# Two transformer layers on one core: late down-weight splits behind the last gate tile, three modulation units a pair, the residual's copy issued by GpSimd

## Chip, core and metric

One Trainium2 chip, one of its cores. The kernel is one launch; the metric is device time in microseconds, the median of repeated runs. A core has five engines that run their own instruction queues strictly in order: TensorE (PE, with its weight loads shown as PEld), VectorE (DVE), ScalarE (ACT), GpSimd (POOL) and SyncE (SP, which here only issues DMAs). They wait for each other by semaphores.

## The reference

Two layers of a diffusion backbone with 512 latent tokens and 256 context tokens, 1024 features. Each layer modulates a normalised stream by vectors made from a conditioning vector, attends, projects, adds a gated residual, and then does the same with a SwiGLU of 2816 hidden features. The second layer gives no context output. Cut to what matters here:

```python
for l in range(DEPTH):                       # 2 layers
    sh_a, sc_a, g_a, sh_f, sc_f, g_f = split(silu(c) @ mod_w[l] + mod_b[l], 6)
    # the context stream has the same six from c_ctx
    a_lat, a_ctx = modulate(h_lat, sh_a, sc_a), modulate(h_ctx, csh_a, csc_a)
    o_lat, o_ctx = mixer(a_lat, a_ctx)       # layer 0: two kinds of heads; layer 1: sliding window
    h_lat = h_lat + g_a * o_lat
    h_lat = h_lat + g_f * swiglu(modulate(h_lat, sh_f, sc_f), w_gate_up[l], w_down[l])
    # the context stream likewise in layer 0 only
return rms_norm(h_lat, final_norm)

def swiglu(h, w_gate_up, w_down):
    g, u = split(h @ w_gate_up, 2)
    return (silu(g) * u) @ w_down
```

## The kernel before

**Layout and precision.** Activations lie transposed: 128 features on the partitions, tokens along the free dimension, so a stream is 8 tiles of 128 x 768 (latent tokens 0 to 511, context 512 to 767). Every float32 operand of a matmul is split into a rounded high part (a cast on ACT) and the rest (a subtraction on DVE), and a product is three matmuls: high x high, high x low, low x high. So each weight panel costs a DMA, a cast and a split before TensorE can use it: `load_w` (cast L311, split L312) or `parts` (cast L1248, split L1249).

**Who sets the order.** The program is written in the order of the mathematics; a planner that simulates a timeline then gives each engine its queue, earlier program text having the higher priority. `behind` (an ordering dependency that costs no semaphore) fixes the order of two instructions of one engine by hand. What the planner has fixed, the engine obeys: if the first instruction of its queue waits for a DMA, everything behind it waits.

**Buffers.** Tiles come from tagged pools with a fixed number of buffers, taken in the order of the program: `wr` (raw weights, 3), `wh`, `wl` (their split, 3 each), `nb` (2), `st` (12), `b` (24), `p` (8), `rope0` (1). A load into a tag goes out when the buffer's last readers are done.

**Layer 0's FFN.** `ffn` walks 22 pairs (gate and up panel j of 128 hidden features) in chunks of 4, 4, 4, 4, 3, 3; after a chunk come its down products for all eight output panels m. Pairs 0 and 1 are plain; the others (`Pair`) use a seven-product scheme in which tokens (halves of 384) and feature halves are combined. Pair j's `head` and `body` come first, then the `tail` of the pair before, so a tail closes a gate tile: two products of 12 matmuls (L1261 to L1263), the Silu on ACT (L1316), the add (L1318), two times gate x up (L1320) on DVE, and cast and split (L1248, L1249) of the hidden tile, which the down products read.

**Modulation units.** Behind pair j stand `bg(more(j))` units of the generator `all_mods`. The first four in the FFN are column products of layer 0's last vector (`mods_pe`), in pairs 0 to 3. The next 48 are layer 1's tiles (`mod_tile` in its late form): POOL issues a load of 128 x 1024 into the one `rope0` buffer (L215), DVE multiplies and sums it against the conditioning vector (L220), for the first 16 tiles twice (both streams).

**The last chunk.** Pairs 19, 20, 21. `final0` fetches the old residual (8 loads by POOL, L1116) and calls `output`: for m = 0 to 7 it gets a down panel of 128 x 384 by `kept_w` (raw in `wr`, split in `nb` for m = 0 and 1, in `st` after that), does nine matmuls for the latent tokens (L322, L324, L325), and the residual's add on DVE (L1112); then the same panels for the context tokens. The sums of squares for layer 1's norm run along (ACT L356, adds L359 on POOL and DVE), then the sum over partitions on TensorE (L373), the root on ACT (L375), the spread (L382) and the modulation (L407 to L409). `kept_w` also loads the first three panels of layer 1's input projection into the list `soon` (L311, L312).

**Behind it.** The latent residual is written to HBM (`parked`, eight DMAs of 256 KB, L1413) so that its buffers can be used; layer 1's key, value and first query products (L763 to L765) follow, and the rotary embedding, whose multiplications run on POOL (L456 to L458).

Of the kernel before, what the change touches and what calls it, by code (L numbers as in the profile page):

```python
# [12 lines left out]
ALU = mybir.AluOpType  # L13

P = 128
D = 1024
KT = D // P
# [10 lines left out]
CHUNKS = ((0, 4), (4, 4), (8, 4), (12, 4), (16, 3), (19, 3)), ((0, 3), (3, 3), (6, 4), (10, 4), (14, 4), (18, 4))  # L28
MLA_SCALE = 96.0 ** -0.5
LOWEST = -3.0e38  # L30
LATS = slice(0, NL)
# [37 lines left out]
LOWER = 150  # L69
LOE = {(0, 2, 0): None, (0, 2, 1): None, (0, 5, 0): None, (0, 5, 1): 1, (1, 2, 0): None, (1, 2, 1): None, (1, 5, 0): None, (1, 5, 1): None}  # L70
PATTERN = ("fbsfbsfbbsfs",) * 3
BG = ((0, 0, 0, 0, 0), (2, 3), (0, 0), (0, 0))
FIRST = 2000
STEPS = ((2, 3, 4, 4), 5, 3)
HALVES = (slice(0, 256), slice(256, 512))
# [25 lines left out]
def hybrid_kernel(ctx: ExitStack, tc, I, out):  # L101
# [6 lines left out]
    def T(tag, shape, dt=F32):  # L108
        count[0] += 1
        if tag not in SIZES:  # L110
            return sb.tile(shape, dt, tag=tag, name=f"{tag}_{count[0]}", bufs=BUFS.get(tag, 1))
        n = int(np.prod(shape[1:]))
        t = sb.tile([P, SIZES[tag] // (2 if dt == mybir.dt.bfloat16 else 4)], dt, tag=tag, name=f"{tag}_{count[0]}",
                    bufs=BUFS[tag])[: shape[0], :n]
        if len(shape) == 3:
            t = t.rearrange("p (a b) -> p a b", a=shape[1])
        return t

    def B(dt=F32, tag="b"):
        return T(tag, [P, NT], dt)  # L120
# [12 lines left out]
    def dma(o, i):  # L133
        return nc.sync.dma_start(f(o), f(i))

    V, S, G, PE = nc.vector, nc.scalar, nc.gpsimd, nc.tensor

    def f(ap):
        return ap.bitcast(F32) if ap.dtype == F32R else ap
# [155 lines left out]
    def bg(n=1):  # L295

        for _ in range(n):
            next(mods, None)
# [7 lines left out]
    def load_w(src, kt, m, eng=None, tag=None, after=()):  # L306

        r = T("wr", [P, kt * m])
        dma(r, src)
        h, lo = (B(F32R, tag)[:, : kt * m] if tag else T(x, [P, kt * m], F32R) for x in ("wh", "wl"))  # L310
        behind(S.copy(h, r), *after[:1])  # L311
        behind((G if eng else V).tensor_tensor(lo, r, f(h), op=ALU.subtract), *after[1:])  # L312
        return tuple(x.rearrange("p (k m) -> p k m", k=kt) for x in (h, lo))
# [48 lines left out]
    marks = {}  # L362
# [75 lines left out]
    def modulated(src, l, comp, eng=None, two=None):  # L438

        res, done = [], []  # L440

        def use(k, r, c, v):
            if k == len(res):
                res.append((B(F32R), B(F32R)))
            done.append(modulate(res[k], src[k], k, r, l, comp, v, c, eng, done[-2:-1]))

        return Norm(src, use, eng, two=two), res
# [72 lines left out]
    def behind(ins, *before):  # L520

        for x in before:
            tc.add_manual_dep(ins.ins, x.ins.name, mybir.DependencyInfo(mybir.DependencyClass.NoSync,
                              mybir.DependencyReason.DATA), reason="products in one run")
        return ins
# [227 lines left out]
    r = B(tag="nb")  # L753
# [78 lines left out]
    def beside(gen):  # L832
        side_work.append(gen)
        return gen
# [79 lines left out]
    def split_pair(p):  # L914

        tag = ("b", "st")[p - 2]
        q, k = raws[2 * p - 4 : 2 * p - 2]
        how = S.copy, G.tensor_copy, V.tensor_copy
        sets.append((new_q(tag), new_k(tag)))
        put_q(sets[p][0], None, how[RQ[p - 2]], (G, V)[RL[p - 2]])(q, slice(0, NT))  # L920
        yield
        put_k(sets[p][1], KC[1], how[RK[p - 2]])(k, slice(0, NT))
        yield
# [63 lines left out]
    def latent_operands(h):  # L987
        p, s = divmod(h, 2)
        r, u = NOPE[s], USED[s]
        rr = slice(32 * (h % 4), 32 * (h % 4) + 32)  # L990
        if p < 2:
            if p == 0:
                KA.append([T("st", [P, NT], F32R) for _ in range(2)])
            QA[s].append([T("st", [P, NT], F32R) for _ in range(2)])
            for t in [*(KA[s] if p == 0 else ()), *QA[s][p]] if s else ():
                (V if "z" in EV else G).memset(f(t[:32]), 0.0)
            if p == 0:
                for i in range(2):
                    V.tensor_copy(KA[s][i][ROPE[s]], KR[i][:32])
        (ka, kc), (qa, qb) = KA[s], QA[s][p % 2]  # L1000
        for x, (hi, lo) in ((kn[p], (ka, kc)), (qn[p], (qa, qb))):
            S.copy(hi[r], x[r])
            (V if "l" in EV and p < 1 else G).tensor_tensor(lo[r], x[r], f(hi[r]), op=ALU.subtract)
        for t, x in zip((qa, qb), QR[h // 4]):
            if "d" in EV:
                dma(t[ROPE[s]], x[rr])
            else:
                G.dma_start(t[ROPE[s]], x[rr])

        def scores(o, q, keys):  # L1010
            q = slice(q * P, (q + 1) * P)
            PE.matmul(o, qa[u, q], ka[u, keys], start=True, stop=False)
            PE.matmul(o, qb[u, q], ka[u, keys], start=False, stop=False)
            PE.matmul(o, qa[u, q], kc[u, keys], start=False, stop=True)

        return scores
# [12 lines left out]
    def na_jobs():  # L1029
        for p in range(4):  # L1030
            if p == 3:
                lower[0] = L3
            for x in ORDER[p]:
                beside(split_pair(int(x)) if x in "23" else {"n": latent_norms, "m": mla_prepare}[x]())
            rate[0] = STEPS[0][p], BG[0][p]
            if p % 2 == 0:
# [34 lines left out]
    def mla_jobs():  # L1071
        phase[0], lower[0] = 1, LOWER
        rate[0] = STEPS[1], BG[0][4]
        ready.append(latent_operands(1))
# [23 lines left out]
    H = []  # L1098
    for k in range(KT):
        t = B()  # L1100
# [13 lines left out]
    def fetched(m, c, tag="p"):  # L1114
        t = B(tag=tag)
        G.dma_start(t[:, c], home[m][:, c])  # L1116
        return t

    ahead, soon = {}, []

    def kept_w(src, m):

        if 2 < m < 6:
            soon.append(load_w(I["w_in1"][(8, 9, 0)[m - 3]], KT, P))
        if m in ahead:
            return ahead[m]
        r, t = T("wr", [P, 384]), T("nb", [P, NT], F32R) if m < 2 else B(F32R, "st")
        dma(r, src(m))
        return tuple(x.rearrange("p (k m) -> p k m", k=3) for x in parts(r, t[:, :384], t[:, 384:]))

    def output(src, mov, l, comp, streams, norm, units, dst=None, keep=False, base=None, wait=0):

# [112 lines left out]
        return Norm(src, use, G if l else None, (0, 4, 1, 5, 2, 6, 3, 7)), ops, sums  # L1245

    def parts(t, h, lo, after=()):
        S.copy(h, t)  # L1248
        behind(V.tensor_tensor(lo, t, f(h), op=ALU.subtract), *after)  # L1249
        return h, lo  # L1250

    norm, ops, sums = combined(H, 0, 3, TOK1, TOK2)
    output(lambda m: I["w_out0"][m], O, 0, 2, ((TOK2, 0), (TOK1, 0)), norm, BG[2])

# [105 lines left out]
    def ffn(l, ops, sums, cs, tags, own, more, down, final):  # L1360

        for ci, (k0, kc) in enumerate(CHUNKS[l]):
            hs, last = [], None
            for j in range(k0, k0 + kc):
                if j == 0:
                    hs.extend(first_pairs(l, ops, cs, tags, own))
                    if l == 0:
                        bg(1)
                    sums()
                elif j >= DIRECT[l]:  # L1370
                    p = Pair(l, j, ops, cs, tags[j - k0], (near_done[3],) if j == DIRECT[l] and l == 0 else ())
                    p.head()
                    if last:
                        last.tail()
                    p.body()
                    hs.append(p.dst)
                    last = p
                bg(more(j))
            src = lambda m: I["w_dn"][l, m, :, k0 * P : (k0 + kc) * P]
            ahead.clear()  # L1380
            ahead[0] = load_w(src(0), kc, P) if l or ci < len(CHUNKS[l]) - 1 else kept_w(src, 0)
            if last:
                last.tail()
            if ci < len(CHUNKS[l]) - 1:
                for m in range(KT):
                    down(m, lambda: ahead.get(m) or load_w(src(m), kc, P), hs)
            else:
                final(src, hs)

    new = []  # L1390
    norm1, A = modulated(new, 1, 0, G, LATS)
# [9 lines left out]
    def final0(src, hs):  # L1401
        new.extend(B() for _ in range(KT))
        old = [fetched(m, slice(0, NT), "b") for m in range(KT)]
        output(src, hs, 0, 5, STREAMS0, norm1, BG[3], new, kept_w, lambda m, c: old[m], 1)

    ffn(0, ops, sums, (TOK1, TOK2), ("st", "st", "b", "b"), norm.marks[0], lambda j: BG[1][j > 9] if j > 3 else j > 1, down0, final0)
    H = new


    parked = []  # L1410
    for k in range(KT):
        t = dr.tile([P, NL], F32, name=f"parked{k}")
        behind(S.dma_start(t, H[k][:, LATS]), norm1.marks[0]["root"])  # L1413
        parked.append(t)
    rope1 = T("rope0", [P, 2, NL])
    dma(rope1, I["rope1"])
# [72 lines left out]
    H = []  # L1489
    for k in range(KT):  # L1490
        t = B()
# [19 lines left out]
    def final1(src, hs):  # L1511
        keep = lambda src, m: ahead.get(m) or load_w(src(m), len(hs), P, None, "b")
        output(src, hs, 1, 5, STREAMS1, Norm(H, finished, G if EF else None), (0, 0), None, keep, wait=1)

    ffn(1, ops, sums, HALVES, ("st",) * 4, norm.marks[0], lambda j: 0, down1, final1)


# [102 lines left out]
```

## Time and profile before

| | us |
|---|---|
| median of 3 runs | 1618.11 (1617.18 to 1618.54) |
| profiled execution, its own time | 1615.98 |
| its span | 1614.2 |
| TensorE busy | 1541.5 |
| DVE busy | 1211.5 |
| ACT busy | 809.2 |
| POOL busy | 324.2 |
| mean granted TensorE clock | 0.984 of full |

The profile is one execution; its busy times are of the span, and its own time is the span plus 1.8 us around it. A row of the timeline gives start, duration, engine, line, operation, what it writes and reads, and in brackets how long the engine was idle before it and what ended that. A matmul's duration includes its passage through the array, so the distance from one start to the next is what a matmul takes in a run of them.

### The profile page before, as it was taken

To read this page: it belongs to the slowest core of one execution; us is meant where nothing else is said; L and a number is where in the kernel's file an instruction comes from. 1 tells how busy PE (TensorE), PEld (TensorE's weight loads), DVE (VectorE), ACT (ScalarE), POOL (GpSimd) and SP (SyncE) were. 2 spreads that over 40 slices of the span, in tenths; PEclk is the share of its full clock that TensorE was granted. 3 is DMA by queue.
4 is the path that set the end of the run, shared out by engine and by line. 5 is a ranking of instruction groups with operands and counts; after the bars stand their busy time and mean duration, and the time that the engine had idled before them with its cause. 6 is when DMAs were issued, how large, how long until landed. Compare 5 with 4: busy or idle time off the path is not lost. (4 is left out here: it accounts for less than half of the span.)

```text
span 1614.2 us, 26523 instructions
## 1 busy us (share of the span) xinstructions
PE 1541.5 (95%) x9910; PEld 1367.8 (85%) x9910; DVE 1211.5 (75%) x2428; ACT 809.2 (50%) x1645; POOL 324.2 (20%) x335
## 2 busy tenths in 40 slices
PE   5899989999999999999999997999999999999997
PEld 3677867786899899999999996887879998898997
DVE  5994878667577679696867686779877688687685
ACT  5453586676365334242423244467756544454453
POOL 1550733320011111102121212384003000000002
PEclk8899999999999999999999999999999999999998
DMA  9455242101553454637455666122006133233232
GB/s 338 156 161 170 60 121 82 44 11 43 192 191 103 150 209 160 218 125 260 159 209 210 227 201 232 66 92 79 2 3 195 43 111 128 86 98 113 92 98 86
DMA packets 76890, 214.93 MB, mean 133 GB/s; under 512 B 10196, under 2 KB 17880, under 8 KB 76760
## 3 DMA queue, kind: packets, MB, share of 16 engines
q1 hardware_dynamic: 58584, 142.96, 27.0%
q0 software_dynamic: 15872, 67.12, 11.9%
q10 hardware_dynamic: 2304, 3.15, 0.5%
q8 instruction: 78, 1.28, 0.3%
q14 instruction: 52, 0.43, 0.1%
HBM read 186.97 MB, written 23.07 MB: 130 GB/s over the span
## 5 line engine op out<-in xcount | busy, mean ns | idle before, releaser
L311 ACT CAST wh<-wr 128x1024 fp32r<-128x1024 f32 (+2 forms) x148 | 114.7, 788 | 200.2 <-PE psd L324 36.0
L312 DVE TENSOR_TENSOR wl<-wr,wh 128x1024 fp32r<-128x1024 f32 (+2 forms) x145 | 137.2, 952 | 78.2 <-ACT wh L311 76.5
L359 POOL TENSOR_TENSOR p<-p,p 128x256 f32<-128x256 f32 (+1 forms) x33 | 31.8, 964 | 468.1 <-ACT p L356 467.2
L553 ACT ACTIVATE p<-p,sm 128x512 f32<-128x512 f32 (+3 forms) x144 | 105.0, 730 | 30.1 <-DVE sm L557 28.1
L1261 PE MATMUL pss<-b,wh 128*128 128x384 f32 (+1 forms) x344 | 107.1, 312 | 0.6 <-ACT b L348 0.6
L1262 PE MATMUL pss<-b,wh 128*128 128x384 f32 (+1 forms) x344 | 107.3, 312 | 0.1
L1263 PE MATMUL pss<-b,wl 128*128 128x384 f32 (+1 forms) x344 | 106.0, 311 | 0.0
L220 DVE CUSTOM_DVE_ANT_0 p<-rope,cond 128x1024 bf16<-128x1024 f32 x64 | 77.2, 1222 | 35.3 <-DMA rope<-in_mod_w_dram 35.0
L324 PE MATMUL psd<-b,wh 128*128 128x512 f32 (+3 forms) x256 | 87.8, 343 | 0.0
L547 PE MATMUL pso<-ph,b 128*64 128x256 f32 (+1 forms) x384 | 77.3, 359 | 3.4 <-DVE ph L485 3.3
L322 PE MATMUL psd<-b,wh 128*128 128x512 f32 (+3 forms) x216 | 77.9, 360 | 1.1 <-ACT b L486 1.0
L547 PE MATMUL pso<-pl,b 128*64 128x256 f32 (+1 forms) x384 | 76.9, 359 | 0.2 <-DVE pl L485 0.2
L325 PE MATMUL psd<-b,wl 128*128 128x512 f32 (+3 forms) x216 | 76.3, 353 | 0.1
L215 POOL DMA_DIRECT2D rope<-in_mod_w_dram x48 | 25.5, 530 | 239.7 <-DVE mod L220 227.3
L1261 PE MATMUL pst<-b,wh 128*128 128x384 f32 (+1 forms) x224 | 69.8, 312 | 0.0
L1262 PE MATMUL pst<-b,wh 128*128 128x384 f32 (+1 forms) x224 | 69.8, 312 | 0.0
L1263 PE MATMUL pst<-b,wl 128*128 128x384 f32 (+1 forms) x224 | 69.7, 311 | 0.0
L322 PE MATMUL pss<-st,wh 128*128 128x512 f32 (+2 forms) x200 | 68.4, 342 | 1.1 <-ACT st L1063 0.9
L325 PE MATMUL pss<-st,wl 128*128 128x512 f32 (+2 forms) x200 | 68.6, 344 | 0.1
L324 PE MATMUL pss<-b,wh 128*128 128x256 f32 (+3 forms) x211 | 68.1, 323 | 0.1
L1261 PEld LDWEIGHTS pss<-b,wh 128*128 128x128 f32 x344 | 64.8, 189 | 1.2 <-ACT b L348 0.9
L747 PE MATMUL pss<-st,st 128*128 128x256 f32 (+3 forms) x194 | 60.3, 331 | 5.8 <-DVE sm L557 5.5
(608 smaller groups left out, 5478.3 us busy)
## 6 DMA issues: line engine op xcount, KB each, us to landing
wr<-in_w_gu_dram SPq DMA_DIRECT2D x88, 512.0 KB, 4.1
rope<-in_mod_w_dram POOLq DMA_DIRECT2D x48, 512.0 KB, 3.8
wr<-in_w_out_dram SPq DMA_DIRECT2D x32, 512.0 KB, 3.9
wr<-in_w_dn_dram SPq DMA_DIRECT2D x64, 256.0 KB, 2.9
p<-home POOLq DMA_DIRECT2D x40, 384.0 KB, 5.4
home<-p POOLq DMA_DIRECT2D x40, 384.0 KB, 4.6
wr<-in_w_in_dram SPq DMA_DIRECT2D x21, 512.0 KB, 3.6
ph<-in_mod_w_dram SPq DMA_DIRECT2D x24, 256.0 KB, 3.4
```

Source lines behind the costliest of these rows:

```text
L220: V.tensor_tensor_reduce(out=T("p", [P, D], mybir.dt.bfloat16), in0=w, in1=cond[:, v, :], op0=ALU.mult, op1=ALU.add, scale=1.0, scalar=0.0 ...
L311: behind(S.copy(h, r), *after[:1])
L312: behind((G if eng else V).tensor_tensor(lo, r, f(h), op=ALU.subtract), *after[1:])
L322: ins = PE.matmul(o, wh[:, k], mh[:, c], start=first and k == 0, stop=False)
L324: PE.matmul(o, wh[:, k], ml[:, c], start=False, stop=False)
L325: PE.matmul(o, wl[:, k], mh[:, c], start=False, stop=last and k == n - 1)
L547: ins = PE.matmul(o[64 * i : 64 * i + 64, c], v(kt), t, start=n == 0, stop=n == len(moving[i]) - 1)
L553: S.activation(p[:, c], p[:, c], AF.Exp, bias=nm, scale=-1.0, accum_out=dn)
L747: PE.matmul(o, x, ks[0][:, keys], start=True, stop=False)
L1261: PE.matmul(o, wh, xh, start=first and k == 0, stop=False, skip_group_check=not first)
L1262: PE.matmul(o, wh, xl, start=False, stop=False, skip_group_check=not first)
L1263: PE.matmul(o, wl, xh, start=False, stop=k == 3, skip_group_check=not first)
```

## The change

Four edits. The number of modulation units behind pairs 4 to 9 of layer 0 becomes 3, as it is behind the later ones. Before the last pair's tail in the last chunk, panels m = 0 and m = 1 are loaded and split, where it was m = 0 alone. For m = 2 to 7 the cast is ordered behind the tail's last cast and the split behind its last split, and layer 1's three panels are loaded in the calls for m = 5, 6, 7, behind the down panel, with the same two orders, where they were loaded in the calls for m = 3, 4, 5 ahead of it. The parked copies go out from POOL, without the order behind the norm's root, where they went out from ACT behind that root.

```diff
-BG = ((0, 0, 0, 0, 0), (2, 3), (0, 0), (0, 0))
+BG = ((0, 0, 0, 0, 0), (3, 3), (0, 0), (0, 0))
...
-    ahead, soon = {}, []
+    ahead, soon, tails = {}, [], []
 
     def kept_w(src, m):
 
-        if 2 < m < 6:
-            soon.append(load_w(I["w_in1"][(8, 9, 0)[m - 3]], KT, P))
         if m in ahead:
             return ahead[m]
         r, t = T("wr", [P, 384]), T("nb", [P, NT], F32R) if m < 2 else B(F32R, "st")
         dma(r, src(m))
-        return tuple(x.rearrange("p (k m) -> p k m", k=3) for x in parts(r, t[:, :384], t[:, 384:]))
+        h, lo = t[:, :384], t[:, 384:]
+        behind(S.copy(h, r), *tails[:1])
+        behind(V.tensor_tensor(lo, r, f(h), op=ALU.subtract), *tails[1:])
+        if m > 4:
+            soon.append(load_w(I["w_in1"][(8, 9, 0)[m - 5]], KT, P, after=tails))
+        return tuple(x.rearrange("p (k m) -> p k m", k=3) for x in (h, lo))
...
     def parts(t, h, lo, after=()):
-        S.copy(h, t)
-        behind(V.tensor_tensor(lo, t, f(h), op=ALU.subtract), *after)
+        marks["cast"] = S.copy(h, t)
+        marks["split"] = behind(V.tensor_tensor(lo, t, f(h), op=ALU.subtract), *after)
         return h, lo
...
             ahead.clear()
-            ahead[0] = load_w(src(0), kc, P) if l or ci < len(CHUNKS[l]) - 1 else kept_w(src, 0)
+            if l or ci < len(CHUNKS[l]) - 1:
+                ahead[0] = load_w(src(0), kc, P)
+            else:
+                ahead.update({m: kept_w(src, m) for m in range(2)})
             if last:
                 last.tail()
+                tails[:] = [marks["cast"], marks["split"]]
...
         t = dr.tile([P, NL], F32, name=f"parked{k}")
-        behind(S.dma_start(t, H[k][:, LATS]), norm1.marks[0]["root"])
+        G.dma_start(t, H[k][:, LATS])
         parked.append(t)
```

## The prediction

> **What bounds the kernel now.** I read the page's totals first, then busy time by stage, then TensorE's waits, then each engine in order of time where those waits lie.
>
> ```profile
> PE 1541.5 (95%) x9910; PEld 1367.8 (85%) x9910; DVE 1211.5 (75%) x2428; ACT 809.2 (50%) x1645; POOL 324.2 (20%) x335
> ```
>
> TensorE (PE) is busy in 95% of the span, 1614.2 us, so little but its gaps can be won. After the start, it is least busy here (length, then busy us of PE, weight load, DVE, ACT, POOL, then clock, DMA share, GB/s):
>
> ```profile
> 960.00:980.00 20.00, 18.39 (x101) 17.35 (x99) 15.29 (x27) 8.20 (x16) 2.11 (x4) 1.00 0.48 159
> 980.00:1000.00 20.00, 14.59 (x61) 11.71 (x60) 9.34 (x18) 4.32 (x8) 4.76 (x9) 0.92 0.96 361
> ```
>
> This is the end of layer 0's FFN: gate tile 21 (the last pair), then the last down products. TensorE's waits between 900 and 1010 us (total, times, longest):
>
> ```profile
> PE pst L322 <- ACT b L1248: 3.3, 1, 3.3
> PE pss L373 <- DVE p L359: 2.7, 1, 2.7
> PE psd L322 <- DVE p L1318: 2.1, 1, 2.1
> PE pst L1261 <- ACT p L1308: 1.6, 1, 1.6
> ```
>
> Three of the four belong to tiles 20 and 21; the 2.7 is the norm's behind them. VectorE and ScalarE in order of time say why (start, duration, instruction, idle time before it and what ended it):
>
> ```profile
> 970.97 1.23 DVE L220 CUSTOM_DVE_ANT_0 p<-rope,cond 128x1024 bf16<-128x1024 f32 x1 [3.58 <-DMA rope<-in_mod_w_dram]
> ...
> 989.37 0.55 DVE L1320 TENSOR_TENSOR p<-p,p 128x384 f32<-128x384 f32 x1
> 989.84 0.55 DVE L1249 TENSOR_TENSOR st<-wr,st 128x384 fp32r<-128x384 f32 x1
> 990.30 0.55 DVE L1318 TENSOR_TENSOR p<-psd,p 128x384 f32<-128x384 f32 x1
> ```
> ```profile
> 974.74 0.46 ACT L1308 COPY p<-pst 128x384 f32<-128x384 f32 x1
> ...
> 985.15 0.51 ACT L1248 CAST st<-wr 128x384 fp32r<-128x384 f32 x1 [2.39 <-DMA wr<-in_w_dn_dram]
> 985.57 1.04 ACT L311 CAST wh<-wr 128x1024 fp32r<-128x1024 f32 x1
> 986.52 0.48 ACT L1316 ACTIVATE p<-pst 128x384 f32<-128x384 f32 x1
> ...
> 993.19 0.51 ACT L1248 CAST st<-wr 128x384 fp32r<-128x384 f32 x1 [4.22 <-DMA wr<-in_w_dn_dram]
> 993.61 0.51 ACT L1248 CAST b<-p 128x384 fp32r<-128x384 f32 x1
> 995.34 0.51 ACT L1248 CAST b<-p 128x384 fp32r<-128x384 f32 x1 [1.23 <-DVE p L1320]
> ```
>
> Both engines are in order and stand at the head of their queues for data still in flight. DVE waits 3.58 us for a modulation tile, and the copy that TensorE needs (974.74) comes late behind it. ACT waits 2.39 and 4.22 us for down weights, and behind those stand tile 21's Silu (986.52) and its last casts (993.61, 995.34). TensorE over the same stretch:
>
> ```profile
> 981.59 0.33 PE L1261 MATMUL pst<-b,wh 128*128 128x384 f32 x1
> ...
> 985.75 0.46 PE L322 MATMUL pss<-st,st 128*128 128x512 f32 x1
> ...
> 998.47 0.63 PE L324 MATMUL pst<-b,nb 128*128 128x512 f32 x1
> ...
> 1002.44 0.40 PE L322 MATMUL pst<-st,st 128*128 128x512 f32 x1
> ...
> 1004.52 0.28 PE L322 MATMUL psd<-st,nb 128*128 128x256 f32 x1
> ```
>
> Tile 21's 24 closing products run from 981.59 to 985.75, 0.173 us each. Panel 7's nine latent down products run from 1002.44 to 1004.52, 0.231 each; there the latent down products end.
>
> **Splits behind the last gate tile, layer 1's panels later.** Cast and split of panels 2 to 7 must now follow tile 21's last cast and split on their engines, so neither engine stands for a down weight before tile 21 is through.
>
> Without its 1.61 us stall TensorE could have gone on at about 973.6 (the stalled product follows the copy's end, 974.74 + 0.46). From there to 1004.52 it did 36 gate products (tile 21's last three groups), 36 x 0.173 = 6.2 us, and 66 of the 72 latent down products (two groups of three lay earlier), 66 x 0.231 = 15.2 us: 21.4 of 30.9 us. The other 9.5 us are the three stalls and products slowed after the longest (0.63 at 998.47, later 0.40).
>
> Not all of it comes back, for the products that filled the time wait too. Before, panels 2 to 5 ran their first products around tile 21's end; now only panels 0 and 1 can. The undisturbed length of a tile's end shows at gate tile 7, on DVE and ACT:
>
> ```profile
> 651.85 0.56 DVE L1318 TENSOR_TENSOR p<-pss,p 128x384 f32<-128x384 f32 x1 [0.40 <-PE pss L1263]
> ```
> ```profile
> 653.38 0.51 ACT L1248 CAST b<-p 128x384 fp32r<-128x384 f32 x1 [1.38 <-DVE p L1320]
> ```
>
> From L1318's start to the cast's end are 2.0 us, with 0.2 for the hand-over 2.2 us of idle TensorE. Removed 9.5, added 2.2: **-7.3 us**. Against it stand two prices of the new order.
>
> (a) The panels' arrival (KB, median us to landing), and the issues of panels 5 to 7 now:
>
> ```profile
> wr<-in_w_dn_dram SPq DMA_DIRECT2D x32, 192.0 KB, 2.7
> ...
> wr<-in_w_in_dram SPq DMA_DIRECT2D x21, 512.0 KB, 3.6
> ```
> ```profile
> 980.20 6.42 SPq L134 DMA_DIRECT2D wr<-in_w_dn_dram  x3
> ```
>
> The wr buffers are three, taken in the order of loading: 2, 3, 4, 5, first layer-1 panel, 6, second, 7, third. The first three are held until tile 21 is through: 973.6 + 36 x 0.173 + 6 x 0.231 = 981.2 for its products, 983.4 for its last cast, 984 for its split. Panel 5 issues at 984.5, is cast by 987.7 and is needed when panels 0 to 4 are done, 983.4 + 33 x 0.231 = 991.0. Panel 7 follows the split of the first layer-1 panel: 985 + 3.6 + 2.3 (cast, split) + 2.7 + 0.5 = 994.1, needed at 995.2. If each load takes the 6.6 us of panel 7 now (issue about 986.6, cast 993.19, DMA share 0.96), it is 985 + 6.6 + 2.3 + 6.6 + 0.5 = 1001, 5.8 us late. Bounds 0 and +5.8; I take **+0.5**, nearer the medians, since POOL's fetches of the old residual, which crowd this stretch, need no longer queue behind modulation loads.
>
> (b) Two layer-1 panels are now split while the norm's sums form, 1.2 us of DVE each. Bounds 0 and +2.4; I take **+0.6**, because residual adds that come one per 2.1 us of products leave DVE gaps.
>
> [...]
>
> **Three units a pair.** A unit is one 512 KB load by POOL into the only rope0 buffer and a product-sum on DVE (two in the first 16 units).
>
> ```profile
> L220 DVE CUSTOM_DVE_ANT_0 p<-rope,cond x64: 1215/1222/1226, 592.1 to 988.2; 128x1024 bf16<-128x1024 f32 x64
> L215 POOL DMA_DIRECT2D rope<-in_mod_w_dram x48: 527/528/541, 534.7 to 983.3; - x48
> ```
>
> 48 units are 6 pairs x 2 + 12 x 3, and with the change 16 x 3: pairs 20 and 21 lose theirs (the DVE wait at 970.97 is in the 9.5). Product-sums by chunk (pairs 4-7, 8-11, 12-15, 16-18, 19-21) go from 16, 18, 12, 9, 9 to 24, 16, 12, 9, 3: pairs 4 to 7 get 8 x 1.22 = 9.8 us of DVE more.
>
> ```profile
> 600.00:620.00 20.00, 20.00 (x117) 20.00 (x116) 19.60 (x35) 10.45 (x19) 1.59 (x3) 1.00 0.37 119
> ...
> 640.00:660.00 20.00, 20.00 (x116) 18.25 (x115) 10.96 (x23) 4.23 (x9) 4.29 (x8) 1.00 0.61 213
> 660.00:680.00 20.00, 20.00 (x117) 17.64 (x116) 15.63 (x26) 5.54 (x9) 2.70 (x5) 1.00 0.81 286
> ```
> ```profile
> 643.88 0.53 POOL L215 DMA_DIRECT2D rope<-in_mod_w_dram  x1
> ```
>
> In the pairs DVE is full (19.60 of 20), TensorE too, and units cannot come faster than the one buffer turns round; the ninth load goes out at 643.88 and waits for pair 8. So the four more units fall behind it, in the down products of 644 to 680, where DVE has 40 - 26.6 = 13.4 us free for the 9.8. Four pairs with three units each are there already, 12 to 15; their whole wait of TensorE between 800 and 870, and the last load among the down products:
>
> ```profile
> PE pst L324 <- DVE b L1249: 0.5, 1, 0.5
> ```
> ```profile
> 839.74 0.53 POOL L215 DMA_DIRECT2D rope<-in_mod_w_dram  x1
> ```
>
> Those units have one product-sum, mine two. Bounds 0 and +14.3 (four waits of 3.58, nothing hidden); I take **+0.5**.
>
> **Residual's copy by POOL.** Eight issues leave ACT, and their place behind the norm's root:
>
> ```profile
> 1012.73 0.42 ACT L356 ACTIVATE p<-b 128x256 f32<-128x256 f32 x1 [1.87 <-issue]
> ```
> ```profile
> 1037.06 1.44 POOL L456 TENSOR_TENSOR b<-b,rope 128x512 f32<-128x512 f32 x1 [14.58 <-DVE b L454]
> ```
>
> ACT loses 1.87 us there, but what is late are squares of the context norm, and TensorE has products without a gap to 1036. POOL pays 8 x 0.53 = 4.2 us, from 1000 on, as each residual lands; it has 14.58 us free before 1037. An issue can catch one of the norm's adds on POOL: -1 to +1.1 (two issues), I take **0**. Without that cover the 4.2 us would delay layer 1's ropes, which run on POOL. [...]
>
> **The sum.** -7.3 + 0.5 + 0.6 + 0.5 + 0 = **-5.7 us**. The profiled execution took 1615.98 us (span 1614.2 and 1.8 around it): 1610.3. It lies 2.1 below the median of the runs shown, 1618.11, from which I forecast 1612.4. Behind 1004.52 I let everything shift: the norm, layer 1's ropes and its attention hang on those products.
>
> **The rivals.** *The panels become the wait* (a at its bound): -7.3 + 5.8 + 0.6 + 0.5 = -0.4, 1617.7. For it: DMA share 0.96 and 361 GB/s; against: the residual fetches may go earlier. 16%.
> *The third unit stalls pairs 4 to 11* (ends slower): six units more with two sums; where the planner sets a sum on DVE before its load has landed, residual adds queue behind it, banks stay full, TensorE stands up to 3.58 us. It decides from the third such stall on (-6.2 + 3 x 3.58 = +4.5); at four, +8.1, 1626.2. For it: DVE at 19.60 of 20; against: pairs 12 to 15. 13%.
> *The planner lays layer 1 out anew*: everything behind the first moved unit is placed again by the planner's own clock. POOL's chain of ropes from 1037 has no spare time; a rope set behind one more pair of POOL operations of 1.4 us costs 2.8, twice that cancels the gain: 1618.0. 8%.
> *More comes back*: products of panels 0 and 1 cover the 2.2, and the norm follows closer, the 2.7 us wait goes too: -5.7 - 2.2 - 2.7 = -10.6, 1607.5. 10%.
> The forecast itself: 53%. That the edit does not bite is excluded for the order (it is fixed by hand) and for the units (counted).
>
> **How the numbers follow.** About 0.2%, 3.2 us, is what a measurement of this kernel can tell from none. Faster: 0.10 + 0.53 x 0.92 + some 0.05 of the first and third rivals = 0.64. Slower: 0.13 + 0.07 from their bad ends = 0.20. Same: 0.16. The likeliest case alone spans 1609 to 1615. The range runs from 1606.5, just under the fourth rival, to 1621, which takes in the first and third and leaves out most of the second.
>
> **What would show it.** Right: no L220 row after about 960; L1316 and L1318 within 1 us of their products; the last L1248 of a gate tile some 12 us before where it stands now; waits of 3.3, 2.1 and 1.6 replaced by one near 2.2. Wrong: a wait of TensorE for wh by L311 or L1248 on a down panel; waits between 640 and 690; L456 on POOL starting late behind DMA issues.

## The result, and the profile after

The changed kernel takes 1633.82 us (median of 6 runs, 1630.31 to 1638.57) against 1617.04 for the kernel before in the same job: ratio 1.0114 [1.0099, 1.0129]. It is slower by some 17 us, where 5.7 less were forecast, and lies outside the range that was given, 1606.5 to 1621. The profiled execution took 1632.95 us, its span is 1631.2.

Both kernels issue 9910 matmuls, so the n-th one's start can be set against its start before. That gives the table that the rest of this text rests on: how much later (+) than before, in us, each kernel is at six products, and at the span's end. (Worked out from the matmul records; near panels that change places the order differs by a few products, so a single figure is good to about 1 us.)

| kernel (n, and its start before) | 3600, 621 | 3900, 674 | 4350, 752 | 5550, 963 | 5700, 1003 | 5850, 1033 | span |
|---|---|---|---|---|---|---|---|
| changed | +0.6 | +12.6 | +17.5 | +21.1 | +12.7 | +18.6 | +17.0 |
| units_only | +2.7 | +13.4 | +18.5 | +20.3 | +10.7 | +11.0 | +10.1 |
| rope_two | +9.1 | +13.0 | +13.5 | +12.2 | +2.5 | +2.8 | +3.6 |
| units_one_sum | -0.5 | +1.5 | +6.3 | +8.7 | -1.0 | -0.7 | -2.6 |
| units_in_down | +2.9 | +3.8 | +7.4 | +9.1 | -0.5 | -0.2 | -2.0 |
| units_late_down | +4.1 | +4.1 | +4.1 | +8.5 | -1.4 | -1.0 | -2.0 |
| splits_only | +0.2 | +0.2 | +0.9 | +2.7 | +2.0 | +7.0 | +8.7 |
| units_down_splits | +0.1 | +0.6 | +6.2 | +9.5 | +2.7 | +7.5 | +7.0 |
| after_copy_act | +1.2 | +12.0 | +16.3 | +18.7 | +11.9 | +16.7 | +14.9 |

What stands in the second column is there at 560 already, ahead of these units' first product-sum (592 in the kernel before), but for 0.9 us in units_in_down and 0.5 in rope_two. It belongs to the single execution (with rope_two perhaps to its one buffer `p` less); read the differences between columns. For the changed kernel: +12.0 in pairs 4 to 7, +4.9 in pairs 8 to 11, +3.6 to the last pair, -8.4 over the last gate tile and most of the down products, then +5.9 up to layer 1's first products. The sum in the prediction had +0.5, then -7.3 and +1.1.

TensorE's waits in pairs 4 to 11, between 590 and 800 us, where the kernel before has none (the four longest of nine), and then at the end of the FFN, between 960 and 1050 (all; total, times, longest):

```profile
PE pss L325 <- DVE wl L312: 2.7, 1, 2.7
PE pst L324 <- DVE b L1252: 1.8, 2, 1.5
PE psd L325 <- DVE wl L312: 1.5, 1, 1.5
PE pss L322 <- ACT wh L311: 1.3, 2, 0.7
```
```profile
PE pss L373 <- DVE p L359: 2.3, 1, 2.3
PE pst L322 <- ACT st L1128: 1.9, 1, 1.9
PE pst L322 <- ACT b L1251: 1.8, 1, 1.8
PE pst L325 <- DVE st L1129: 1.5, 1, 1.5
```

(Line numbers after the changed places are 3 to 7 higher than in the kernel before: L1251 and L1252 are the cast and split of `parts`, L1128 and L1129 those of `kept_w`, L1319, L1321 and L1323 the Silu, the add and the products.) The waits of 3.3, 2.1 and 1.6 us are gone, as forecast. New ones stand in the pairs, where TensorE had been full, and two on panel 7. Three stretches of 20 us (the first as it was before, then all three now; before, the other two stand in the prediction) show what that costs (length, then busy us of PE, weight load, DVE, ACT, POOL, then clock, DMA share, GB/s):

```profile
620.00:640.00 20.00, 20.00 (x117) 19.91 (x116) 18.13 (x32) 8.81 (x17) 3.19 (x6) 1.00 0.40 127
```
```profile
620.00:640.00 20.00, 18.64 (x105) 17.86 (x105) 15.71 (x27) 8.10 (x15) 1.58 (x3) 1.00 0.32 106
640.00:660.00 20.00, 17.62 (x95) 15.57 (x94) 12.48 (x26) 4.93 (x10) 1.58 (x3) 1.00 0.36 119
660.00:680.00 20.00, 15.80 (x79) 13.04 (x78) 14.15 (x27) 3.42 (x6) 7.47 (x14) 0.91 0.82 303
```

TensorE loses 7.9 us of these 60, and DVE, in its way, is not full either: it is busy for 42.3 of the 60 (44.7 before). It stands, that is, it waits idle at the head of its queue. DVE in order of time (start, duration, idle time before it and what ended that):

```profile
639.09 1.22 DVE L220 CUSTOM_DVE_ANT_0 p<-rope,cond 128x1024 bf16<-128x1024 f32 x1 [3.09 <-DMA rope<-in_mod_w_dram]
...
659.69 1.22 DVE L220 CUSTOM_DVE_ANT_0 p<-rope,cond 128x1024 bf16<-128x1024 f32 x1 [2.06 <-DMA rope<-in_mod_w_dram]
...
660.84 1.22 DVE L220 CUSTOM_DVE_ANT_0 p<-rope,cond 128x1024 bf16<-128x1024 f32 x1
...
661.98 0.55 DVE L1321 TENSOR_TENSOR p<-pss,p 128x384 f32<-128x384 f32 x1
662.45 0.55 DVE L1252 TENSOR_TENSOR b<-p,b 128x384 fp32r<-128x384 f32 x1
...
666.51 1.23 DVE L220 CUSTOM_DVE_ANT_0 p<-rope,cond 128x1024 bf16<-128x1024 f32 x1 [1.90 <-DMA rope<-in_mod_w_dram]
667.66 1.22 DVE L220 CUSTOM_DVE_ANT_0 p<-rope,cond 128x1024 bf16<-128x1024 f32 x1
...
668.80 1.89 DVE L312 TENSOR_TENSOR wl<-wr,wh 128x512 fp32r<-128x512 f32 x3
```

A gate tile's add and split (661.98, 662.45) stand behind 2.06 us of waiting and two product-sums; the splits of the down weights (668.80) behind the next 1.90 and two more. TensorE pays for each at once:

```profile
663.06 0.39 PE L324 MATMUL pst<-b,wh 128*128 128x256 f32 x1 [1.50 <-DVE b L1252]
...
669.55 0.70 PE L325 MATMUL pss<-st,wl 128*128 128x512 f32 x1 [2.65 <-DVE wl L312]
```

Each sum waits for its load, and the load for the sum before it, since there is one buffer. POOL's loads of the units:

```profile
595.26 0.54 POOL L215 DMA_DIRECT2D rope<-in_mod_w_dram  x1 [5.20 <-DVE mod L220]
...
662.36 0.53 POOL L215 DMA_DIRECT2D rope<-in_mod_w_dram  x1 [6.59 <-DVE mod L220]
```

Eleven of them lie from 595.26 to 662.36, one per 6.7 us (a twelfth went out at 535, before them). The twelve units of pairs 4 to 7 thus last until 670, into chunk 2's down products, and there DVE takes the waits at the head of its queue.

### The profile page after: what moved, and what is told of

Same layout as the page of the kernel before. It is cut to its first block, busy times and chain, and to the rows that moved or that the text cites. A ratio compares the mean times of both kernels' runs of the same rounds, so it can differ in the third digit from the quotient of the medians.

```text
span 1631.2 us, 26535 instructions
## 1 busy us (share of the span) xinstructions
PE 1547.8 (95%) x9910; PEld 1368.4 (84%) x9910; DVE 1211.8 (74%) x2428; ACT 806.5 (49%) x1645; POOL 327.7 (20%) x343
## 5 line engine op out<-in xcount | busy, mean ns | idle before, releaser
L312 DVE TENSOR_TENSOR wl<-wr,wh 128x1024 fp32r<-128x1024 f32 (+2 forms) x145 | 137.2, 953 | 84.5 <-ACT wh L311 84.0
L1264 PEld LDWEIGHTS pss<-b,wh 128*128 128x128 f32 x344 | 64.9, 189 | 1.1 <-ACT b L348 0.9
L1265 PEld LDWEIGHTS pss<-b,wh 128*128 128x128 f32 x344 | 65.0, 189 | 0.9 <-DVE b L349 0.6
```

The source lines that it names most:

```text
L1264: PE.matmul(o, wh, xh, start=first and k == 0, stop=False, skip_group_check=not first)
L1265: PE.matmul(o, wh, xl, start=False, stop=False, skip_group_check=not first)
```

## Experiments: the units

**Only the third unit** (the kernel before with the one edit):

```diff
-BG = ((0, 0, 0, 0, 0), (2, 3), (0, 0), (0, 0))
+BG = ((0, 0, 0, 0, 0), (3, 3), (0, 0), (0, 0))
```


> The kernel before with one edit, three modulation units behind pairs 4 to 9. Theory U (the third unit costs the time: modulation loads hold POOL's queue and DVE in the down products of pairs 4 to 11): layer 0's last write-backs of chunks 2 and 3 come 12 and 19 us later, as in the changed kernel, and pairs 20 and 21 without units give back 2 to 4, so 1631 to 1636. Theory S (the split order of the last chunk costs it): within 4 us of 1617.

Measured 1626.62 against 1616.21, ratio 1.0067 [1.0046, 1.0089]. Nearly the whole loss of the pairs is here: +17.6 from 621 to 963, where the changed kernel has +20.5 and after_copy_act +17.5. And the end gives back 9.6 without any order of splits; TensorE's one wait from 960 to 1060 is the norm's:

```profile
PE pss L373 <- DVE p L359: 3.0, 1, 3.0
```

**All but the third unit** (the changed kernel with `(2, 3)`):

> The changed kernel with two units behind pairs 4 to 9 again. Theory U: the 17 us go, and the rest of the change shows: 1611 to 1617, with gate tile 21 closed within 8.2 - 21.2 + (2 to 5 for the units of pairs 20 and 21) = -11 to -8 us of before. Theory S: 1630 or more.

1623.16, ratio 1.0048 [1.0031, 1.0064]: the pairs are as before (+0.6 from 621 to 963), and the end loses 7.4 up to product 5850 instead of gaining. Its recorded theory, 1611 to 1617, did not come true. With units behind pairs 20 and 21 the order of the splits brings waits of its own, 3.4, 3.2 and 2.5 us for casts.

**POOL's queue or DVE's.** Loads of units and fetches of the old residual share POOL's queue, so the loss in the pairs could also come from fetches queued behind loads. units_only with the fetches issued by SP:

```diff
-        G.dma_start(t[:, c], home[m][:, c])
+        nc.sync.dma_start(t[:, c], home[m][:, c])
```


> The kernel before with three units behind pairs 4 to 9, and the residual fetches of the FFN issued by SP instead of POOL. Theory Q (in pairs 4 to 11 the fetches of the old residual stand in POOL's queue behind modulation loads that wait for their product-sums, and hold the down products): the +18 of units_only between pairs 4 and 12 falls below +5, time 1606 to 1613. Theory D (VectorE itself stands for loads that have not landed and is full besides): it stays above +13, time 1624 or more.

1633.88 against 1614.85, ratio 1.0115 [1.0096, 1.0134]; at product 5550 it is at +30.7. Freed from the fetches, POOL's queue brought nothing back. SP's queue, which carries the weights, may have paid for them (TensorE's waits for L312 between 595 and 800 us are 5.6 us, against 2.6 in units_only), so this run speaks against POOL's queue as the main cause only together with rope_two below.

Then the turn of the buffer, both times on top of units_only. First one product-sum a unit (so 1.22 us less of DVE and an earlier next load; this kernel leaves out the context's modulation vectors of layer 1's first norm and uses the latent's there). And, apart from that, two buffers, paid for with one `p`:

```diff
-            for v in vecs:
+            for v in vecs[:1]:
```


> The kernel before with three units behind pairs 4 to 9, and every unit with one product-sum; the context's modulation vectors of layer 1's first norm are left out, the latent's stand in their place. 16 product-sums of 1.22 us go from VectorE, the loads stay. Theory Q: the units still run past the pairs, since a load comes each 5.4 us and 12 of them take 65: half of the +18 stays. Theory D: the +18 falls below +3.

```diff
-BUFS = dict(b=24, part=4, st=12, wr=3, wh=3, wl=3, p=8, ph=4, pl=4, sm=10, nb=2)
+BUFS = dict(rope0=2, b=24, part=4, st=12, wr=3, wh=3, wl=3, p=7, ph=4, pl=4, sm=10, nb=2)
```


> The kernel before with three units behind pairs 4 to 9 and two rope0 buffers instead of one; for the space the p buffers are 7 instead of 8. A load can then land while the tile before it is being summed. Theory D (VectorE stands for loads that have not landed): the waits of VectorE for rope0 in 620 to 700 us go and the +16 of pairs 4 to 11 falls below +6: 1606 to 1614. Theory Q (POOL's queue holds the fetches): it stays above +10, since all units still stand ahead of the fetches: 1620 or more.

units_one_sum: 1615.07, ratio 1.0 [0.9988, 1.0012]; the pairs cost +9.2 instead of +17.6. rope_two: 1617.56, ratio 1.0008 [0.9995, 1.0021]; the same work for DVE as in units_only, the same loads, and pairs 4 to 11 cost +4.4 instead of +15.8, no more than +3.1 up to the last pair. The product-sums between 595 and 693 in the kernel before, units_only, rope_two and units_one_sum (count, busy us, mean ns, idle time before them):

```profile
L220 DVE CUSTOM_DVE_ANT_0 p<-rope,cond 128x1024 bf16<-128x1024 f32 x18 | 21.4, 1219 | 3.2 <-DMA rope<-in_mod_w_dram 3.1
```
```profile
L220 DVE CUSTOM_DVE_ANT_0 p<-rope,cond 128x1024 bf16<-128x1024 f32 x24 | 28.4, 1222 | 13.5 <-DMA rope<-in_mod_w_dram 13.5
```
```profile
L220 DVE CUSTOM_DVE_ANT_0 p<-rope,cond 128x1024 bf16<-128x1024 f32 x24 | 28.5, 1218 | 0.0
```
```profile
L220 DVE CUSTOM_DVE_ANT_0 p<-rope,cond 128x1024 bf16<-128x1024 f32 x13 | 15.9, 1224 | 13.0 <-DMA rope<-in_mod_w_dram 13.0
```

Between 693 and 793 the idle times are 2.9, 11.8, 0.3 and 20.7 us. units_only and rope_two do the same sums; only the standing differs, and without it most of the price is gone. So what the pairs pay for comes from DVE's waits at the head of its queue, for loads that the single buffer makes late: shown, but for the one `p` less in rope_two.

The wait is not the price by itself, though. units_one_sum stands longer than units_only, 33.7 against 25.3 us from 595 to 793, and pays less: 2.0 in pairs 4 to 7 and 4.8 in pairs 8 to 11, against 10.7 and 5.1. And the kernel before stands for 23.0 us before its sums between 793 and 960, while TensorE waits for 1.0. Waits seem to cost where DVE's other work leaves it little time, as with the second sums of pairs 4 to 7; this is argued from these numbers, and no run sets it apart. That about half of the loss stays in units_one_sum is what its theory Q (POOL's queue) had expected, and not D; rope_two, where all units stand ahead of the fetches as in units_only, speaks against Q's reason.

In sum rope_two is no gain: the pairs still pay 3 to 4, and it is 9.1 behind before them.

**The same units elsewhere.** Leave pairs 4 to 9 at two units and set the six that pairs 20 and 21 had among the down products: of chunks 2 and 3 (units_in_down, panels 2, 4, 6), or of chunks 3, 4 and 5, where a unit has one sum (units_late_down, panels 2 and 5):

```diff
+        if 8 <= downs[0] < 24 and m in (2, 4, 6):
+            bg(1)
+        downs[0] += 1
```


> The kernel before with two units behind pairs 4 to 9 as it had, and six more units in the down products of chunks 2 and 3, one behind each of the panels m = 2, 4, 6, so that pairs 20 and 21 have none and no unit is added ahead of the fetches of the old residual. Theory P (it is the place of the added units, ahead of the down products of pairs 4 to 11, that costs 16 us, and the pairs 20 and 21 without units give back 9): 1604 to 1609. Rival L (the added loads and sums cost wherever they are put in those chunks): 1613 or more.

```diff
+        if 16 <= downs[0] < 40 and m in (2, 5):
+            bg(1)
+        downs[0] += 1
```


> The kernel before, with two units a pair behind pairs 4 to 9 and then one unit behind panels 2 and 5 of the down products of chunks 3, 4 and 5, where a unit has one product-sum; none lie behind pairs 20 and 21. Theory: the end gives back 9.6 us as in units_only, units_one_sum, rope_two and units_in_down, and units with one sum, spread over down products that are 24 us long, cost 0 to 3 us instead of the 7 that units_in_down paid: 1606 to 1611. Rival: any unit between the pairs delays what stands behind its load on VectorE, the time is paid back in chunks 3 to 5, and it is 1613 to 1617.

units_in_down: 1614.8 against 1615.16, ratio 0.9994 [0.9982, 1.0007]: +6.2 in the pairs, -9.6 at the end. units_late_down: 1611.56 against 1615.62, ratio 0.9978 [0.9968, 0.9988]: +4.4 and -9.9. It is faster than the kernel before by 0.2%, and the only one here that is; its units cost 4.4, more than the 0 to 3 that its theory gave them. From 600 to 800 us TensorE waits for nothing; after that for 4.0 us ahead of the norm (all waits from 600 to 1060):

```profile
PE pss L373 <- DVE p L359: 3.1, 1, 3.1
PE pst L1263 <- DVE wl L1249: 2.0, 3, 0.9
PE pst L324 <- DVE b L1249: 1.0, 1, 1.0
PE psd L322 <- ACT b L1248: 1.0, 2, 0.7
```

## Experiments: the order of the splits

**Only the order** (the kernel before with the `kept_w`, `parts` and `ahead` parts of the diff):

> The kernel before with the splits of panels 2 to 7 behind the last gate tile, panels 0 and 1 ahead of it and layer 1's panels behind panels 5 to 7; units and the residual's copy as before. Theory U: a gain, but smaller than the 7.3 forecast, since pairs 20 and 21 keep their units and panel 7 waits for a wr buffer: 1612 to 1616. Theory S: slower than 1620.

1622.89, ratio 1.0032 [1.0018, 1.0046]. Of the three stalls of 3.3, 2.1 and 1.6 it leaves 2.6, none and 0.2, and it makes others: TensorE's further waits above 0.5 us from 960 on are 2.6 (the norm's), 1.9, 1.3, 0.9 and 0.8. Panel 7 goes out at 1003.49, when the first layer-1 panel's split has freed its buffer. Panel 5 goes out at 992.05 and is cast 7.8 us later:

```profile
999.85 0.51 ACT L1128 CAST st<-wr 128x384 fp32r<-128x384 f32 x1 [4.74 <-DMA wr<-in_w_dn_dram]
```

Two variants move the layer-1 panels out of the way: all three behind panel 7, or behind the whole last output. A third takes the raw panels out of `wr` into `p` buffers.

```diff
-        if m > 4:
-            soon.append(load_w(I["w_in1"][(8, 9, 0)[m - 5]], KT, P, after=tails))
+        if m > 6:
+            soon.extend(load_w(I["w_in1"][i], KT, P, after=tails) for i in (8, 9, 0))
```


> As splits_only, but all three of layer 1's panels are loaded behind panel 7, so panel 7 no longer waits for a wr buffer that the first of them holds. Theory A (the panels' arrival through the three wr buffers gives the gain back): some 3 us less than splits_only, 1618 to 1621. Theory N (the norm behind them gives it back): as splits_only, 1622 to 1624.

> As splits_only, but layer 1's three panels are loaded in the program behind the whole last output, so neither panel 7 nor the norm's sums share VectorE and ScalarE with them unless these are idle. Theory A and N together (panels in the ring 3 us, their splits in the norm 4 us): 1613 to 1617, TensorE's wait for the norm's sum at 2.7 or less. If the wait for the norm's sum stays near 5: the norm's adds are late for another reason.

```diff
-        r, t = T("wr", [P, 384]), T("nb", [P, NT], F32R) if m < 2 else B(F32R, "st")
+        if m % 2 == 0:
+            raw[:] = [B(tag="p")]
+        r = raw[0][:, 384 * (m % 2) : 384 * (m % 2) + 384]
+        t = T("nb", [P, NT], F32R) if m < 2 else B(F32R, "st")
```


> As splits_panels_last, and the raw down panels of the last chunk lie in p buffers instead of wr, so all can be loaded before gate tile 21 closes; only their casts and splits stand behind it. Theory A: no wait of TensorE for a panel is left, the latent down products end 5 us before those of the kernel before, 1610 to 1614. Theory N: 1617 or more.

splits_panels_last: 1620.57, ratio 1.004 [1.0024, 1.0057]. splits_panels_after: 1620.46, ratio 1.0035 [1.0021, 1.0048]. The latent down products end at 1005.4 and 1007.3, some 4 to 6 us earlier than in splits_only, but no earlier than in the kernel before (1004.5; the two are 0.7 and 2.6 behind it at 963). And the wait before the norm's sum grows to 5.5 and 5.2 us: the panels' splits now lie between the norm's adds on DVE. In splits_panels_after:

```profile
1006.05 1.22 DVE L312 TENSOR_TENSOR wl<-wr,wh 128x1024 fp32r<-128x1024 f32 x1
1007.19 0.69 DVE L359 TENSOR_TENSOR p<-p,p 128x512 f32<-128x512 f32 x1
1007.79 1.22 DVE L312 TENSOR_TENSOR wl<-wr,wh 128x1024 fp32r<-128x1024 f32 x1
...
1009.59 0.68 DVE L359 TENSOR_TENSOR p<-p,p 128x512 f32<-128x512 f32 x1
1010.18 1.22 DVE L312 TENSOR_TENSOR wl<-wr,wh 128x1024 fp32r<-128x1024 f32 x1
```

splits_raw_apart, 1635.14, ratio 1.012 [1.0102, 1.0137], tells nothing of the buffers: the loads go out only between 974 and 1003, presumably because the `p` buffers come free late (not shown), and TensorE waits 7.4 and, in two waits, 7.0 us.

The same move alone, without the order and with units_in_down:

```diff
-        if 2 < m < 6:
-            soon.append(load_w(I["w_in1"][(8, 9, 0)[m - 3]], KT, P))
...
+        soon.extend(load_w(I["w_in1"][i], KT, P) for i in (8, 9, 0))
```


> As units_in_down, and layer 1's three panels loaded behind the whole last output; no order of the splits by hand. Theory P with the panels out of the way: 1603 to 1608. If the panels' place does not matter once pairs 20 and 21 have no units: as units_in_down.

1612.89, ratio 0.9992 [0.9979, 1.0006]: not to be told from no change.

**The order without units in its way.** Last, the whole order on top of units_in_down:

> units_in_down with the whole split order of the change (panels 0 and 1 ahead, the others behind tile 21, the first layer-1 panels with panels 5 to 7). Theory: with no unit left in pairs 20 and 21 nothing stalls there for down weights, so the order can only lose: 4 to 8 us slower than units_in_down, 1618 to 1623, with TensorE waiting for casts or splits of panels 5 to 7. Rival: the order pays once the DVE wait for modulation loads is gone: 1610 to 1614.

1622.22, ratio 1.0041 [1.0027, 1.0056]. Both kernels are at +9.5 and +9.1 when the last pair begins; behind it the one gains 2.0 up to product 5850, the other 9.3. So the order costs 7.3 us here, and the changed kernel loses as much against units_only (-2.5 and -9.3). Its waits are of the same kind as the changed kernel's: 1.8 for tile 21's last cast, 1.9 for panel 7's split, 2.3 before the norm's sum.

## Experiments: the residual's copy

The copy alone, and the changed kernel with the copy back on ACT behind the root:

```diff
-        behind(S.dma_start(t, H[k][:, LATS]), norm1.marks[0]["root"])
+        G.dma_start(t, H[k][:, LATS])
```


> The kernel before with one edit, the residual's eight copies issued by POOL without the order behind the norm's root. Both theories: within 1.5 us of 1617. If POOL's issues catch the norm's adds or layer 1's ropes: 1619 to 1622.

> The changed kernel with the copy of the residual back on ScalarE behind the norm's root. If the copy by POOL costs there what it cost alone (+4), this is 1628 to 1631. If in the changed kernel the residuals' last adds come so far apart that POOL's issues fit between (its wait before the norm's sums is 2.3 us, not 5.4), this is 1632 to 1635.

copy_only: 1620.21, ratio 1.0026 [1.0014, 1.0038], some 4 us slower. Before, POOL's three adds for the norm follow each other in 4.35 us. Now eight issues stand ahead of and between them:

```profile
1002.95 1.21 POOL L1413 DMA_DIRECT2D parked<-b  x2 [11.86 <-DVE b L1112]
1004.22 1.29 POOL L359 TENSOR_TENSOR p<-p,p 128x512 f32<-128x512 f32 x1
1005.47 1.62 POOL L1413 DMA_DIRECT2D parked<-b  x3
1007.11 1.58 POOL L359 TENSOR_TENSOR p<-p,p 128x512 f32<-128x512 f32 x1
1008.64 1.62 POOL L1413 DMA_DIRECT2D parked<-b  x3
1010.28 1.27 POOL L359 TENSOR_TENSOR p<-p,p 128x512 f32<-128x512 f32 x1
```

DVE waits 2.34 us for the last of them, and TensorE's wait before the norm's sum is 5.4 instead of 2.7. In the changed kernel the same edit costs nothing that shows: after_copy_act took 1632.06, ratio 1.0108 [1.0089, 1.0126], against 1.0114 with the copy on POOL; from the last pair to product 5850 it gains 2.0 and the changed kernel 2.5, and the norm's wait is 2.3 in both. The late panels space the residuals, and an issue falls where POOL waits anyway:

```profile
1011.51 0.54 POOL L1420 DMA_DIRECT2D parked<-b  x1 [1.39 <-DVE b L1112]
1013.29 0.54 POOL L1420 DMA_DIRECT2D parked<-b  x1 [1.25 <-DVE b L1112]
1013.85 1.30 POOL L359 TENSOR_TENSOR p<-p,p 128x512 f32<-128x512 f32 x1
```

## Why the prediction was wrong

**Three units a pair, +0.5 taken, +20.5 measured (17.5 to 17.6 in after_copy_act and units_only): the step that failed.** The prediction set the 9.8 us of additional sums against 13.4 us that DVE had free in the down products. It priced the sums' busy time, and counted free time as if DVE could choose. But a sum comes with the wait before it: the prediction itself had the load period of one buffer, and still let the ninth to twelfth unit lie "where DVE has 13.4 us free". A DVE that was idle for a load, 2.06 us ahead of 659.69 and 1.90 ahead of 666.51, held up the splits behind it as a busy one would. The bound of +14.3 covered pairs 4 to 7 (measured +12.0); it left out pairs 8 to 11 (+4.9), where by the prediction's own count there are two sums fewer, but DVE stands longer, and the rest (+3.6). The analogue, pairs 12 to 15 with a TensorE wait of 0.5, has one sum a unit and a load every 5.5 us. DVE stands there too (23.0 us between 793 and 960) and TensorE hardly feels it, so it did not carry. Two such loads of before, from pairs 20 and 21 (POOL in order of time):

```profile
977.92 0.53 POOL L215 DMA_DIRECT2D rope<-in_mod_w_dram  x1 [4.90 <-DVE mod L220]
983.29 0.53 POOL L215 DMA_DIRECT2D rope<-in_mod_w_dram  x1 [4.85 <-DVE mod L220]
```

units_one_sum shows how much of the price hangs on the second sum. The second rival described this mechanism, in-order sums ahead of their loads, with its place and its sign; what queues behind the sums are splits above all, where it named residual adds, and pairs 4 to 11 get six units more and six sums more (34 to 40), not six units with two sums. At 13% its chance was too small, and the range left it out.

**The three stalls, -7.3 taken.** The size was right, the cause was not. The 9.5 us that the prediction read out of the stretch from 973.6 to 1004.52 all come back, 9.6 to 9.9 us from product 5550 to 5700 in each of the seven runs without units behind pairs 20 and 21 and without the order (units_only, units_fetch_sp, units_one_sum, rope_two, units_in_down, units_late_down, units_down_panels_after). The prediction took ACT's standing for down weights (2.39 and 4.22 us) as a cause of its own that the order would cure. In units_only ACT still stands for them, though shorter, and TensorE does not feel it:

```profile
999.39 0.52 ACT L1248 CAST st<-wr 128x384 fp32r<-128x384 f32 x1 [2.10 <-DMA wr<-in_w_dn_dram]
```

What of a unit does the harm there is not settled: the DVE wait of 3.58 us is gone, and the residual's fetches go out earlier too (from 970.50 in units_only, with everything 20 us late, against 983.81 before). With them out of the way the last down panels land sooner: after a median of 2.5 us in units_only (issues from 994 to 1004), against 4.9 before (979 to 995). No run takes the two apart. Tile 21's last split (995.88 before) was to come some 12 us earlier. It comes at 1004.12, with the 21.1 taken off 12.9 earlier; but 10.1 of that are there in units_only as well (1006.06, less 20.3), and the rest is of no use. The hand-over at the tile's close was forecast at 2.2 us and is 1.78; the 0.2 in it beside the engines' 2.0 was the author's estimate: here 0.04 us lie ahead of the add (1002.39) and 0.05 behind the cast (ended 1004.09). It is a price that only the order pays: without it the first products of panels 2 to 5 fill that time. The prediction said so and still called the rest a gain of the order.

**Panels' arrival and layer-1 splits, +0.5 and +0.6 taken.** Panel 5 came in time, as (a) said. Panel 7 did not, and not for its transfer alone. It goes out at 1012.37, behind the split that frees its buffer; then its cast stands behind one of the norm's squares, which itself waits 1.13 us for a residual add, and its split behind layer 1's split and a norm's add:

```profile
1015.92 1.05 ACT L311 CAST wh<-wr 128x1024 fp32r<-128x1024 f32 x1 [0.28 <-DMA wr<-in_w_in_dram]
1018.10 0.63 ACT L356 ACTIVATE p<-b 128x512 f32<-128x512 f32 x1 [1.13 <-DVE b L1112]
1018.64 0.49 ACT L1128 CAST st<-wr 128x384 fp32r<-128x384 f32 x1
```
```profile
1017.98 1.22 DVE L312 TENSOR_TENSOR wl<-wr,wh 128x1024 fp32r<-128x1024 f32 x1
1019.11 1.77 DVE L359 TENSOR_TENSOR p<-p,p 128x512 f32<-128x512 f32 x1
1020.81 0.55 DVE L1129 TENSOR_TENSOR st<-wr,st 128x384 fp32r<-128x384 f32 x1
```

TensorE waits 1.9 for the one and 1.5 for the other, and the products behind them are slow (0.63 us each instead of 0.40, up to 1024.5). From product 5700 to 5850 the changed kernel loses 5.9, units_only 0.3: the size of the first rival (+5.8), only in part by its path, the load. The terms were counted as free engine time and as the ring of `wr` alone; the queue order on ACT and DVE between the two was not.

**Copy by POOL, 0 taken.** Right in the changed kernel, by luck: alone it costs 4, beyond the bound of +1.1, because six issues, and not two, stand between the norm's adds when residuals come close together.

**The sum, then:** +20.5 (units, pairs 4 to 19), -9.6 (units, end), +7 (order), 0 (copy), with the execution's own +0.6 and -1.6 behind product 5850: 16.9 of the span's 17.0.

## What to carry to other kernels

When work is moved to an in-order engine, price the wait that comes with each piece and list what stands behind it; here 13.4 us of free time in a window were no cover for 9.8 us of sums that waited for transfers through a single buffer (pairs 4 to 7 paid 12.0). How much of such a wait is paid depends on what stands behind it: here between almost nothing and nearly all. When several waits cluster, look for one cause upstream before ordering the late work by hand: here moving six units cured waits in three places, and the order added waits of its own. The six units cost least in late down products, one sum each: 0.2% faster than before.

## What was not expected of the hardware

TensorE's clock fell after waits shorter than the 3.29 us (up to 995.90) behind which it fell in the kernel before (0.50 from 998 to 1000). After 2.65 us (669.55; a wait of 1.50 lies 4 us ahead of it) matmuls took 0.63 instead of 0.40 for 3.5 us, at a granted clock of 0.52 from 669.55 to 673.05; after 1.78 us (1004.14) they did not, with a clock of 1.00 from 1004 to 1008, nor after 2.12 before (991.00); after 1.91 and 1.49 with two matmuls between they did (0.50 from 1021.41 to 1024.50):

```profile
1021.41 0.79 PE L325 MATMUL pst<-st,st 128*128 128x512 f32 x1 [1.49 <-DVE st L1129]
...
1024.13 0.63 PE L325 MATMUL pst<-b,st 128*128 128x512 f32 x1
```

What sets the clock these runs do not show. POOL's eight issues of 256 KB in the changed kernel took 0.54 to 0.56 us each between 1007 and 1026 us, where DVE was busy for 13.0 of the 19 us, much as the 0.53 of the modulation loads; what they cost in copy_only is their place in POOL's queue.
